# Query rope's weights in the pairs' ring, projections by halves, and the first weights on another queue

## The chip, the cores and the metric

The kernel runs on one core of one Trainium2 chip. The metric is the device time of one execution in microseconds. Five engines run their own instruction streams: TensorE (PE, matmuls; PEld is its weight load), VectorE (DVE), ScalarE (ACT), GpSimd (POOL) and SyncE (SP, which mostly issues DMAs). They meet through semaphores. Matmuls read from SBUF and write to PSUM banks, and a bank can be written again only when its last reader is done.

## The reference

Input x is 1024 tokens by 1024 features. Layer 1 is a gated linear recurrence, layer 2 is attention whose keys and values come from one shared low-rank projection. All in float32. In outline:

```python
# layer 1
u = rms_norm(x) @ w_in;  xb, gate = split(u)            # 1280 + 1280
xb = causal_conv(xb);    r, i = sigmoid gates per block of 128
h = associative_scan(exp(-8 r softplus(-lam)), ...)
x = x + (h * silu(gate)) @ w_out
# shared keys and values
ckr = rms_norm(x) @ w_dkv;  c_kv = rms_norm(ckr[:256]);  k_rope = rope(ckr[256:])
k_nope, v = c_kv @ w_uk, c_kv @ w_uv                    # 8 heads of 128
# layer 2
u = rms_norm(x) @ w_in;  c_q = rms_norm(u[:384]);  gate = u[384:]
q = c_q @ w_uq;  q_nope, q_rope = q[:128], rope(q[128:])  # per head
o = causal softmax(scale * (q_nope k_nope + q_rope k_rope)) @ v
x = x + (o * silu(gate)) @ w_out;  out = rms_norm(x, final_norm)
```

## The kernel before, in words

**Three matmuls for one product.** Every float32 operand is split into a high part (rounded for the fast matmul format) and a low part: the helper `hl` (lines 81 to 83) rounds on ACT (L82) and subtracts on DVE (L83). A product is the sum of three matmuls, high by high, high by low, low by high (`mm3`, L114 to L116). Tiles `wh`, `wl` are the parts of a weight, `pg` is a page of 128 by 1024 (one of 36), `wr` the raw weight, `ps` and `pm` PSUM banks, `s` the scores' banks, `pt` the transposed probabilities.

**The start.** Eighteen small matmuls on ones (L285) keep PE running until data are there. SP, ACT and DVE follow a hand-written order here (`manual_schedule`): SP issues the halves of x's first pages (`xload`, L245) and the first weights (`Weights.load`, L267) in turn; ACT loads its function table (L288), then scales and splits each piece of x (L252, DVE's half is L253) and adds up the squares (L275, L277, DVE L149); the sum reaches PE as the matmul of L359.

**The pairs.** From about 365 to 525 us, the projections into keys, queries and gates run as products of two row blocks at a time in Strassen's manner: `pair` makes seven products (`fmul`) of 12 matmuls into four banks a, b, c, d, where copies of banks (`copy`, ACT L634) start other banks: b starts from a's content, cc keeps c, d starts from b, v2 keeps b. Differences go through DVE (L654). Each pair's weights come from four loads of winc (L526) into the ring `wa` of 7 buffers; ACT scales each by four small instructions (L530), DVE adds them to each other (L542), and `hl` splits them into rings `wh` and `wl` of 4. The instructions of a pair's weights and its copies carry a priority (WPRI or WPC, 100 and 120) with which the scheduler places them ahead in the engines' queues; the queues themselves run strictly in order. Query rope (`qrope`) needs four weights of its own (wuqr, 192 KB); they use the general ring `wr` of 2 buffers (`wtile`, L91). The gates' pairs 0, 2, 4 and 6 follow each other, query rope stands after gates pair 2.

**The heads.** From about 527 us, eight heads of eight query blocks each: scores (five matmuls for each piece of 512, L890 to L894) into one of two banks `s`; mask and row maximum on DVE (L895, L897), exponential on ACT (L900), normalisation on DVE (L901, L902); transposes on PE (L910) that are split again into `pt`; and for each half of the queries the product with the values (`pv`, L925 to L927), multiplied by the gate on DVE (L929). The next head's projections `kq` are cut into four pieces, q first and second half, then k first and second half, which a table (KQ_AT, by query block) spreads between the blocks as filler. PVD says how many blocks after its half `pv` is placed: 1, but 3 for the second part of head 6. The last projection and the final norm follow from about 785 us.

Of the kernel before, what the change touches and what calls it, by code (L numbers as in the profile page):

```python
# [10 lines left out]
F32R = mybir.dt.float32r  # L11
# [10 lines left out]
NH = 8  # L22
# [11 lines left out]
DEPQ = "gpsimd"  # L34
LOOK = 2
KQ_AT = (1, 0, 1, 0, 2, 0, 0, 0)
V0_AT = (1, 1, 2, 0)
V_AT = (0, 0, 0, 0, 0, 0, 1, 1)
D_AT = (0, 4, 1, 1, 1, 0, 3, 2)
# [10 lines left out]
GADD = ()  # L50
NWA = 7
WPC = 120


NA, CW, CB, BR, BI, LAM, NKV, KVN, NB, QN, FN, NVEC = 0, 8, 48, 58, 68, 78, 88, 96, 98, 106, 109, 117
# [2 lines left out]
def trunk(tc, xT, wina, vecs, wgate, wouta, winc, wuk, wuv, wuq, wuqr, woutb, rope, outT):  # L58
# [196 lines left out]
    class Weights:  # L255
# [6 lines left out]
            self.lo = wp.tile([P, 4 * P], F32R, tag="wl", bufs=4, name=nm("wl"))  # L262
            ks += [(self.hi[:, k * P:(k + 1) * P], self.lo[:, k * P:(k + 1) * P]) for k in range(4)]

        def load(self, k0=0, k1=4):
            c = slice(k0 * P, k1 * P)
            nc.sync.dma_start(out=self.raw[:, c], in_=self.src[:, c])  # L267

        def split(self, k0=0, k1=4):
            c = slice(k0 * P, k1 * P)  # L270
# [14 lines left out]
        T.matmul(out=warm[:, 0:P], lhsT=onesd, rhs=onesd, start=True, stop=True)  # L285
    rb = accp
    with tc.manual_schedule(engines={_E.SP, _E.Activation, _E.DVE}):
        A.activation(out=atab, in_=onesd[:, 0:1], func=AF.Abs_reciprocal_sqrt)  # L288
        sp = softplus()

        def step(n):
            for _ in range(n):
                next(sp, None)

        w0 = [Weights(wina[j][:, 0:4 * P], w) for j, w in ((0, wx), (NCT, wg))]
        xload(0, hs(0))
        w0[0].load(0, 1)
        w0[1].load(0, 1)
        xload(0, hs(1))
        w0[0].load(1, 4)  # L300
        xload(1, hs(0))
        w0[1].load(1, 4)
        xload(1, hs(1))
        xload(2)
        xload(3)
        step(SPN[0])
        xsplit(0, hs(0))
        w0[0].split(0, 1)
        w0[1].split(0, 1)
        xsplit(0, hs(1))  # L310
        ps0 = [pst() for _ in range(4)]

        def products(k):
            for i in range(4):
                mm3(ps0[i], (wx, wg)[i // 2][k], (xs[k][0][:, hs(i % 2)], xs[k][1][:, hs(i % 2)]), k == 0, k == NKT - 1)

        def first(k):

            for h in range(2):
                for wp_, xp in ((0, 0), (0, 1), (1, 0)) if (k, h) == (0, 0) else ((0, 0), (1, 0), (0, 1)):  # L320
                    for i in range(2):
                        T.matmul(out=ps0[2 * i + h], lhsT=(wx, wg)[i][k][wp_], rhs=xs[k][xp][:, hs(h)],
                                 start=k + wp_ + xp == 0, stop=False)

        first(0)
        w0[0].split(1, 4)
        xsplit(1, hs(0))
        w0[1].split(1, 4)
        xsplit(1, hs(1))
        w4 = [Weights(wina[j][:, 4 * P:], w) for j, w in ((0, wx), (NCT, wg))]  # L330
        for w in w4:
            w.load()
        for k in range(4, NKT):
            xload(k)
        first(1)
        done = 0
        for k in range(2, NKT):
            xsplit(k)
            step(SPN[1])
            if k == 3:  # L340
                for w in w4:
                    w.split()
            products(k)
            while done <= k - SQL:
                squares(done)
                step(SPN[1])
                done += 1
        for k in range(done, NKT):
            squares(k)
        ws = wload(wgate[0], 2 * P, tag="s", pool=ta, rb=1, hb=1)  # L350
        wx = wtile(wina[1], NKT, cast=True)
        ap = [(tt(F32R), tt(F32R)) for _ in range(2)]
        for h in range(2):
            hl(accp[:, hs(h)], *ap[h])
        for h in range(2):
            t1, t2 = tt(), tt()
            ps = pst()
            for i in range(2):
                T.matmul(out=ps, lhsT=onesr, rhs=ap[h][i], start=i == 0, stop=i == 1)  # L359
            newton(rb[:, hs(h)], ps, 1.0 / D, t1, t2)  # L360
        step(99)
# [264 lines left out]
    def pair(m, dst, w, banks, raw=(False, False), mid=None):  # L626

        a, c, b, d = banks
        cc = tcp.tile([P, HW], F32, tag="cc", bufs=2, name=nm("cc"))
        v2 = tcp.tile([P, HW], F32, tag="v2", name=nm("v2"))  # L630

        def copy(dst_, src, scale=1.0):
            with tc.high_priority(offset=WPC):
                A.activation(out=dst_, in_=src, func=AF.Copy, scale=scale)  # L634

        fmul(a, w[0], 0, True)
        copy(b, a, -1.0)
        fmul(c, w[1], 1, True)
        copy(cc, c)
        fmul(b, w[2], 2, False)  # L640
        fmul(a, w[3], 4, False)
        copy(d, b)
        copy(v2, b)
        fmul(d, w[4], 3, False)
        rest = mid() if mid else None

        def put(i, h, src):
            if raw[i]:
                A.activation(out=dst[i][h], in_=src, func=AF.Copy)
            else:  # L650
                byr(dst[i][h], src, r1[:, hs(h)])

        def put2(i, h, x, y):
            V.tensor_tensor(out=dst[i][h], in0=x, in1=y, op=ALU.subtract)  # L654
            if not raw[i]:
                byr(dst[i][h], dst[i][h], r1[:, hs(h)])

        put2(1, 1, d, cc)
        put(0, 0, a)
        fmul(c, w[5], 6, False)  # L660
        put2(0, 1, c, v2)
        fmul(d, w[6], 5, False)
        put(1, 0, d)
        if rest:
            rest()

    def wa():
        return tcp.tile([P, HW], F32, tag="wa", bufs=NWA, name=nm("wa"))
# [108 lines left out]
    qsd = dp.tile([4, 2 * P, S], F32, name="qsd")  # L777

    def qrope(g):
        wab = [wtile(wuqr[2 * g + i], 3) for i in range(2)]  # L780
        for h in range(2):
            pA, pB = pst(), pst()
            mmt(pA, wab[0], cq, hs(h))
            mmt(pB, wab[1], cq, hs(h))
            for c, (o1, o2, op) in enumerate(((cs, sn, ALU.subtract), (sn, cs, ALU.add))):
                t1, t2 = tk(), tk()
                V.tensor_tensor(out=t1, in0=pA, in1=o1[:, hs(h)], op=ALU.mult)
                V.tensor_tensor(out=t2, in0=pB, in1=o2[:, hs(h)], op=ALU.mult)
                V.tensor_tensor(out=t1, in0=t1, in1=t2, op=op)
                th, tl = parts(t1, t2.bitcast(F32R))  # L790
                DQ.dma_start(out=qsd[c, g * P:(g + 1) * P, hs(h)], in_=f(th))
                DQ.dma_start(out=qsd[2 + c, g * P:(g + 1) * P, hs(h)], in_=f(tl))
# [47 lines left out]
    def kq(hd):  # L840

        wk, wq = wtile(wuk[hd], 2), wtile(wuq[hd], 3)
        k, q = (page(), page()), (page(), page())
        qs = tp.tile([P, S], F32R, tag="qs", name=nm("qs")) if hd else page()
        for c in range(4):
            nc.sync.dma_start(out=f(qs[32 * c:32 * c + 32, :]), in_=qsd[c, 32 * hd:32 * hd + 32, :])

        def proj(w, src, dst, h):
            ps = pm()
            mmt(ps, w, src, hs(h))  # L850
            hl(ps, dst[0][:, hs(h)], dst[1][:, hs(h)])

        work = [lambda a=a, h=h: proj(*a, h) for a in ((wq, cq, q), (wk, ckv, k)) for h in range(2)]
        return (k, q, qs), work

    def vals(pair, half):
# [124 lines left out]
    for i, (hd, qb) in enumerate(items):  # L981
        if qb == 0:
            gt = page(F32)
            nc.sync.dma_start(out=gt, in_=gd[hd])
            gates.append(gt)
            if hd + 1 < NH:
                heads[hd + 1], kqwork = kq(hd + 1)
        if qb == VQB and hd // 2 + 1 < NH // 2:
            vwork += vals(hd // 2 + 1, hd % 2)
        if i + LOOK < len(items):  # L990
            nh = items[i + LOOK]
            if nh[1] == 0 and nh[0]:
                while kqwork:
                    kqwork.pop(0)()
            pend[nh] = scores(*nh, *heads[nh[0]])
        if i == 8 * (NH - 1) + DSTART:
            dwork = [lambda a=a: dpart(*a) for a in DPART]
        for wl, n in ((kqwork, KQ_AT[qb]), (vwork, V0_AT[qb] if hd == 0 and qb < 4 else V_AT[qb]), (dwork, D_AT[qb - DSTART] if i >= 8 * (NH - 1) + DSTART else 0)):
            for _ in range(min(n, len(wl))):
                wl.pop(0)()  # L1000
        g = qb // 4
        if qb % 4 == 0:
            pts[hd, g] = [tuple(tp.tile([P, 4, HW], F32R, tag=f"pt{i}", name=nm("pt")) for i in range(2)) for _ in range(g + 1)]

        if late and i - late[0][0] >= (PVD if (hd, qb) < (NH - 2, 4) or hd == NH - 1 else 3):
            pv(*late.pop(0)[1:])
        transposes(qb, pend.pop((hd, qb)), pts[hd, g])
        if qb % 4 == 3:
            late.append((i, hd, g, pts.pop((hd, g))))
        j = i - 8 * (NH - 1)  # L1010
        for _ in range(YL_AT.count(j)):
            yload(ny)
            ny += 1
        for _ in range(WOUT_AT.count(j)):
            wout(len(wob))
# [131 lines left out]
```

## Time and profile before

| | |
|---|---|
| median of 3 runs | 873.49 us (873.47 to 873.86) |
| the profiled execution's own time | 873.94 us |
| its span, first to last instruction | 872.2 us |
| PE busy | 856.4 us, 4326 matmuls |
| DVE busy | 660.7 us |
| ACT busy | 519.1 us |
| granted clock of TensorE | 0.996 |

The span is 1.74 us shorter than the execution's own time; what lies around it is outside the profile. Rows of a timeline read: start, length, engine, line, operation, output and inputs, shape, and in brackets how long the engine had been idle and what released it. PE's rows show modelled ends: a matmul of 512 columns is shown with 0.39 us though the next starts 0.23 us after it.

### The profile page before, as it was taken

What the parts mean: (1) busy time and instruction counts of PE and PEld (TensorE: products, weight loads), DVE (VectorE), ACT (ScalarE), POOL (GpSimd) and SP (SyncE); (2) the same over time, 40 slices, a digit from 0 to 9 for tenths busy, and PEclk for the clock granted to TensorE, in tenths of its full rate; (3) what the DMA queues carried; (4) which work ended last, traced back from release to release, by engine and by line L of the source; (5) the groups of instructions that cost most, each with busy time, mean ns of one, the idle gap of its engine ahead of it and who ended that gap; (6) DMA issues with size and microseconds to landing.
All of it is one profiled execution on the core that took longest, in us unless ns stands there. A gap on an engine that the chain in (4) does not pass through costs nothing.

```text
span 872.2 us, 12195 instructions
## 1 busy us (share of the span) xinstructions
PE 856.4 (98%) x4326; PEld 728.3 (84%) x4326; DVE 660.7 (76%) x1227; ACT 519.1 (60%) x961; POOL 73.3 (8%) x143
## 2 busy tenths in 40 slices
PE   9999999999999999999999999999999999999995
PEld 6788888888888888888778889988998998888995
DVE  6988788777877774779878957887797887875353
ACT  7567787776787543699875545555565554431222
POOL 1001110011000100001211320000000000010000
PEclk9999999999999999999999999999999999999998
DMA  8333333333212544133544674122231326666032
GB/s 294 94 97 97 97 96 98 107 100 95 79 37 91 169 151 158 49 109 122 182 138 170 204 257 133 52 83 96 70 112 67 105 74 249 217 211 216 14 130 75
DMA packets 52222, 109.00 MB, mean 125 GB/s; under 512 B 6593, under 2 KB 17217, under 8 KB 52161
## 3 DMA queue, kind: packets, MB, share of 16 engines
q1 hardware_dynamic: 36400, 67.19, 23.7%
q0 software_dynamic: 15216, 40.51, 13.9%
q8 instruction: 34, 0.56, 0.3%
q10 hardware_dynamic: 544, 0.52, 0.2%
q14 instruction: 28, 0.22, 0.1%
HBM read 81.46 MB, written 26.21 MB: 123 GB/s over the span
## 4 chain that ended last, share of the span: by engine, by line
PE 88%; DVE 4%; ACT 3%; DMA 2%; issue 2%; SPq 0%; POOL 0%; DVEq 0%; ACTq 0%; POOLq 0%
PE ps L114 16%; PE ps L116 16%; PE ps L115 16%; PE pm L116 6%; PE pm L115 6%; PE pm L114 6%; PE pm L910 3%; PE pm L926 2%; PE pm L927 2%; PE s L891 2%; PE pm L925 2%; PE s L893 2%; PE s L894 2%; PE s L892 2%; PE s L890 2%
## 5 line engine op out<-in xcount | busy, mean ns | idle before, releaser
L114 PE MATMUL ps<-pg,wh 128*128 128x512 f32 x664 | 257.1, 390 | 3.3 <-ACT ps L634 2.4
L115 PE MATMUL ps<-pg,wh 128*128 128x512 f32 x664 | 258.7, 390 | 0.6 <-DVE pg L253 0.5
L116 PE MATMUL ps<-pg,wl 128*128 128x512 f32 x664 | 258.4, 389 | 0.0
L114 PEld LDWEIGHTS ps<-pg,wh 128*128 128x128 f32 x664 | 124.6, 188 | 31.0 <-ACT ps L634 3.6
L115 PEld LDWEIGHTS ps<-pg,wh 128*128 128x128 f32 x664 | 124.6, 188 | 27.7 <-DVE pg L253 1.9
L116 PEld LDWEIGHTS ps<-pg,wl 128*128 128x128 f32 x664 | 124.6, 188 | 25.9
L82 ACT ACTIVATE pt<-pm 128x512 fp32r<-128x512 f32 (+2 forms) x96 | 44.3, 490 | 59.4 <-PE pm L910 54.5
L900 ACT ACTIVATE pg<-s,m 128x128 f32<-128x128 f32 (+3 forms) x64 | 47.4, 742 | 45.1 <-DVE m L897 40.4
L114 PE MATMUL pm<-pg,pg 128*128 128x256 f32 (+1 forms) x192 | 61.9, 322 | 0.0
L115 PE MATMUL pm<-pg,pg 128*128 128x256 f32 (+1 forms) x192 | 61.6, 321 | 0.0
L116 PE MATMUL pm<-pg,pg 128*128 128x256 f32 (+1 forms) x192 | 61.4, 320 | 0.0
L83 DVE TENSOR_TENSOR pt<-pm,pt 128x512 fp32r<-128x512 f32 (+2 forms) x96 | 50.5, 548 | 2.3 <-ACT pt L82 2.2
L897 DVE TENSOR_REDUCE m<-s 128x1 f32<-128x128 f32 (+3 forms) x64 | 48.2, 754 | 1.1
L82 ACT ACTIVATE wh<-wr 128x512 fp32r<-128x512 f32 (+3 forms) x59 | 31.2, 531 | 26.0 <-PE ps L115 15.2
L83 DVE TENSOR_TENSOR wl<-wr,wh 128x512 fp32r<-128x512 f32 (+3 forms) x59 | 33.1, 564 | 16.1 <-ACT wh L82 15.9
L381 DVE SCALAR_TENSOR_TENSOR t<-xb,vec,t 128x512 f32<-128x512 f32 x60 | 44.8, 747 | 0.4
L82 ACT ACTIVATE pg<-pg 128x512 fp32r<-128x512 f32 x42 | 26.1, 630 | 30.0 <-DVE pg L435 18.3
L910 PE MATMUL pm<-ident,pg 128*128 128x128 f32 x288 | 42.3, 274 | 0.7 <-DVE pg L929 0.7
L116 PE MATMUL pm<-pg,wl 128*128 128x512 f32 x108 | 42.3, 392 | 0.0
L115 PE MATMUL pm<-pg,wh 128*128 128x512 f32 x108 | 42.3, 392 | 0.0
L114 PE MATMUL pm<-pg,wh 128*128 128x512 f32 x108 | 42.1, 390 | 0.0
L114 PEld LDWEIGHTS pm<-pg,pg 128*128 128x128 f32 x192 | 36.6, 191 | 2.6 <-issue 0.2
(232 smaller groups left out, 1803.4 us busy)
## 6 DMA issues: line engine op xcount, KB each, us to landing
wr<-wina SPq DMA_DIRECT2D x38, 256.0 KB, 2.9
wh<-wina POOLq DMA_DIRECT2D x36, 256.0 KB, 2.9
wa<-winc SPq DMA_DIRECT2D x24, 256.0 KB, 3.1
ysd<-pg POOLq DMA_DIRECT2D x12, 512.0 KB, 3.2
pg<-ysd SPq DMA_DIRECT2D x12, 512.0 KB, 8.9
wr<-wouta SPq DMA_DIRECT2D x16, 256.0 KB, 2.7
t<-xT SPq DMA_DIRECT2D x16, 256.0 KB, 3.4
x1d<-t POOLq DMA_DIRECT2D x16, 256.0 KB, 2.5
```

The source lines that it names most:

```text
L82: A.activation(out=hi, in_=src, func=AF.Copy)
L83: V.tensor_tensor(out=lo, in0=src, in1=f(hi), op=ALU.subtract)
L114: T.matmul(out=ps, lhsT=w[0], rhs=r[0], start=first, stop=False, skip_group_check=more)
L115: T.matmul(out=ps, lhsT=w[0], rhs=r[1], start=False, stop=False, skip_group_check=more)
L116: T.matmul(out=ps, lhsT=w[1], rhs=r[0], start=False, stop=last, skip_group_check=more)
L381: V.scalar_tensor_tensor(out=xc, in0=xb[:, j:j + HW], scalar=cwv[j], in1=xc, op0=ALU.mult, op1=ALU.add)
L890: T.matmul(out=sc[:, c], lhsT=q[0][:, ql], rhs=k[0][:, c], start=True, stop=False)
L891: T.matmul(out=sc[:, c], lhsT=q[0][:, ql], rhs=k[1][:, c], start=False, stop=False)
L892: T.matmul(out=sc[:, c], lhsT=q[1][:, ql], rhs=k[0][:, c], start=False, stop=False)
L897: V.tensor_reduce(out=m, in_=sc, axis=AX.X, op=ALU.max, negate=True)
L900: A.activation(out=p_[:, 0:nk], in_=sc, func=AF.Exp, bias=m, accum_out=l)
L910: T.transpose(out=ps[:, (b - b0) * P:(b - b0 + 1) * P], in_=p_[:, b * P:(b + 1) * P], identity=ident)
```

## The change

Four edits, all of order and placement; the matmuls are the same.

1. The first two weight loads (64 KB each) are issued by ACT, ahead of its table load, and no longer by SP between the pieces of x.
2. The copies of banks in `pair` get priority 600 in place of 120.
3. Query rope's weights are taken from the pairs' ring `wa`, by code that repeats `wtile`'s split.
4. A head's projections come as q, k of the first half, then q, k of the second. For the last head, the second halves are left until after its first scores (table KQ_LAST), and `pv` stands one block after its half everywhere.

```diff
+KQ_LAST = (1, 0, 0, 0, 1, 0, 1, 1)
+WPB = 600
...
-        def load(self, k0=0, k1=4):
+        def load(self, k0=0, k1=4, q=nc.sync):
             c = slice(k0 * P, k1 * P)
-            nc.sync.dma_start(out=self.raw[:, c], in_=self.src[:, c])
+            q.dma_start(out=self.raw[:, c], in_=self.src[:, c])
...
+        w0 = [Weights(wina[j][:, 0:4 * P], w) for j, w in ((0, wx), (NCT, wg))]
+        for w in w0:
+            w.load(0, 1, nc.scalar)
         A.activation(out=atab, in_=onesd[:, 0:1], func=AF.Abs_reciprocal_sqrt)
...
-        w0 = [Weights(wina[j][:, 0:4 * P], w) for j, w in ((0, wx), (NCT, wg))]
         xload(0, hs(0))
-        w0[0].load(0, 1)
-        w0[1].load(0, 1)
         xload(0, hs(1))
...
-            with tc.high_priority(offset=WPC):
+            with tc.high_priority(offset=WPB):
                 A.activation(out=dst_, in_=src, func=AF.Copy, scale=scale)
...
     def qrope(g):
-        wab = [wtile(wuqr[2 * g + i], 3) for i in range(2)]
+
+        wab = []
+        for i in range(2):
+            with tc.high_priority(offset=WPRI):
+                raw = wa()[:, 0:3 * P]
+                hi = wp.tile([P, 3 * P], F32R, tag="wh", bufs=4, name=nm("wh"))
+                lo = wp.tile([P, 3 * P], F32R, tag="wl", bufs=4, name=nm("wl"))
+                nc.sync.dma_start(out=raw, in_=wuqr[2 * g + i])
+                hl(raw, hi, lo)
+            wab.append([(hi[:, k * P:(k + 1) * P], lo[:, k * P:(k + 1) * P]) for k in range(3)])
...
-        work = [lambda a=a, h=h: proj(*a, h) for a in ((wq, cq, q), (wk, ckv, k)) for h in range(2)]
+        work = [lambda a=a, h=h: proj(*a, h) for h in range(2) for a in ((wq, cq, q), (wk, ckv, k))]
...
-                while kqwork:
+
+                while len(kqwork) > (2 if nh[0] == NH - 1 else 0):
                     kqwork.pop(0)()
...
-        for wl, n in ((kqwork, KQ_AT[qb]), (vwork, V0_AT[qb] if hd == 0 and qb < 4 else V_AT[qb]), (dwork, D_AT[qb - DSTART] if i >= 8 * (NH - 1) + DSTART else 0)):
+        for wl, n in ((kqwork, (KQ_LAST if hd == NH - 2 else KQ_AT)[qb]), (vwork, V0_AT[qb] if hd == 0 and qb < 4 else V_AT[qb]), (dwork, D_AT[qb - DSTART] if i >= 8 * (NH - 1) + DSTART else 0)):
...
-        if late and i - late[0][0] >= (PVD if (hd, qb) < (NH - 2, 4) or hd == NH - 1 else 3):
+        if late and i - late[0][0] >= PVD:
             pv(*late.pop(0)[1:])
```

Two lines more stand at the kernel's head, so L634 becomes L636, and from `qrope` on the lines move by 11 (L929 becomes L940).

The order on ACT around copy d of the first gates pair (the bank ps_3931, L634; L530 scales a winc tile, `wh_...<-wa_...` splits one). Before:

```order
L634 ACTIVATE cc_3932<-ps_3929 128x512
L82 ACTIVATE wh_3920<-wa_3904 128x512
L530 ACTIVATE wa_4433<-wa_4433,vec 128x128 x4
L82 ACTIVATE wh_3924<-wa_3883 128x512
L634 ACTIVATE ps_3931<-ps_3930 128x512
```

Now:

```order
L636 ACTIVATE cc_3932<-ps_3929 128x512
L84 ACTIVATE wh_3920<-wa_3904 128x512
L84 ACTIVATE wh_3924<-wa_3883 128x512
L636 ACTIVATE ps_3931<-ps_3930 128x512
L636 ACTIVATE v_775_3933<-ps_3930 128x512
```

The four scalings of wa_4433 have left this place; they now stand before the split of wh_4141 that is followed by copy d of gates pair 2 (ps_4148), where those of wa_4602 stood. On SP, the loads of that stretch before:

```order
L526 DMA wa_4121<-winc 128x512
L91 DMA wr_4253<-wuqr 128x384
L526 DMA wa_4433<-winc 128x512
L526 DMA wa_4439<-winc 128x512
L526 DMA wa_4445<-winc 128x512
L526 DMA wa_4466<-winc 128x512
L91 DMA wr_4259<-wuqr 128x384
L526 DMA wa_4602<-winc 128x512
```

Now:

```order
L528 DMA wa_4121<-winc 128x512
L789 DMA wa_4253<-wuqr 128x384
L789 DMA wa_4259<-wuqr 128x384
L789 DMA wa_4341<-wuqr 128x384
L789 DMA wa_4347<-wuqr 128x384
L528 DMA wa_4433<-winc 128x512
L528 DMA wa_4439<-winc 128x512
L528 DMA wa_4445<-winc 128x512
```

All four wuqr loads now stand ahead of the winc loads of gates pair 4 (wa_4433 and on). On PE in head 6, from the end of block 4's scores (s_7196) to the scores of block 5, before:

```order
L894 MATMUL s_7196<-pg_4776,qs_6749 128x256
L114 MATMUL pm_7215<-pg_4062,wh_7101 128x512
L115 MATMUL pm_7215<-pg_4063,wh_7101 128x512
L116 MATMUL pm_7215<-pg_4062,wl_7102 128x512
L114 MATMUL pm_7215<-pg_4068,wh_7101 128x512
L115 MATMUL pm_7215<-pg_4069,wh_7101 128x512
L116 MATMUL pm_7215<-pg_4068,wl_7102 128x512
L114 MATMUL pm_7215<-pg_4074,wh_7101 128x512
L115 MATMUL pm_7215<-pg_4075,wh_7101 128x512
L116 MATMUL pm_7215<-pg_4074,wl_7102 128x512
L910 MATMUL pm_7227<-ident,pg_7124 128x128 x3
L890 MATMUL s_7233<-pg_6745,pg_6747 128x512
```

Now:

```order
L904 MATMUL s_7196<-pg_4775,qs_6749 128x256
L905 MATMUL s_7196<-pg_4776,qs_6749 128x256
L921 MATMUL pm_7215<-ident,pg_7124 128x128 x3
L901 MATMUL s_7221<-pg_6745,pg_6747 128x512
L902 MATMUL s_7221<-pg_6746,pg_6747 128x512
```

The nine matmuls of the second half of q have left this place; with the six of k's second half they follow the first scores of head 7.

## The prediction

> **What bounds the kernel now.** I read the page first, then busy time by stretch, then TensorE's waits, then the timelines around each wait.
>
> ```profile
> span 872.2 us, 12195 instructions
> PE 856.4 (98%) x4326; PEld 728.3 (84%) x4326; DVE 660.7 (76%) x1227; ACT 519.1 (60%) x961; POOL 73.3 (8%) x143
> ...
> PE 88%; DVE 4%; ACT 3%; DMA 2%; issue 2%; SPq 0%; POOL 0%; DVEq 0%; ACTq 0%; POOLq 0%
> ```
>
> TensorE (PE) is busy 98% of the span and 88% of the chain that ended last is its own work. The change removes no matmul, so all it can win is PE's idle time. Where that lies, by stretch (columns: length, then PE, PEld, DVE, ACT, POOL busy, granted clock, DMA share, GB/s):
>
> ```profile
> 1.70:4.60 2.90, 2.90 (x15) 2.90 (x15) 0.90 (x7) 0.95 (x3) 0.00 (x0) 1.00 0.67 197
> 4.60:14.00 9.40, 8.86 (x34) 5.84 (x33) 5.61 (x9) 6.95 (x12) 0.00 (x0) 1.00 0.98 331
> ...
> 427.00:460.00 33.00, 29.66 (x127) 23.25 (x126) 27.59 (x45) 27.05 (x60) 4.37 (x8) 1.00 0.39 127
> 460.00:742.00 282.00, 282.00 (x1592) 248.32 (x1591) 228.47 (x479) 154.78 (x337) 25.77 (x48) 1.00 0.38 130
> 742.00:748.00 6.00, 4.93 (x34) 4.24 (x34) 5.82 (x15) 4.12 (x12) 0.53 (x1) 1.00 1.04 398
> ```
>
> Between 460 and 742 us, as an example of the rest, PE never idles. Where the change works it idles in three places: the start, 427 to 460 us (3.34 us idle: the pairs of products), and 742 to 748 us (1.07 us: the end of head 6). PE's own waits name the releasers:
>
> ```profile
> PE ps L114 <- ACT ps L634: 2.4, 3, 1.1
> ...
> PE ps L114 <- DVE tk L654: 1.0, 1, 1.0
> PE pm L910 <- DVE pg L929: 0.7, 1, 0.7
> ```
>
> So three waits for ScalarE's bank copies (L634), one for VectorE's difference (L654), one for its product with the gate (L929) at the end of head 6. A shown wait is too short, because matmuls of 512 columns start every 0.23 us while a row shows 0.39; I therefore measure a stall from start to start, less 0.23, plus 0.11 because the first row after a stall lasts 0.50 and not 0.39.
>
> **The pairs' stretch, 427 to 460 us.** Timelines of ACT and of PE (start, length, operation, idle before it and its releaser):
>
> ```profile
> 420.90 0.60 ACT L649 ACTIVATE pg<-ps 128x512 f32<-128x512 f32 x1 [1.79 <-DMA kvd<-pg]
> ```
>
> ```profile
> 428.30 0.39 PE L116 MATMUL ps<-pg,wl 128*128 128x512 f32 x1
> 429.67 0.50 PE L114 MATMUL ps<-pg,wh 128*128 128x512 f32 x1 [0.98 <-ACT ps L634]
> ```
>
> Stall A, 1.37 − 0.23 + 0.11 = 1.25 us, is the first gates pair's copy b. It runs late because ACT was held 1.79 us by a spill to DRAM (kvd). The change moves nothing ahead of that, so I leave A: 0, at best −0.6 if the spill lands early.
>
> ```profile
> 434.16 1.28 ACT L530 ACTIVATE wa<-wa,vec 128x128 f32<-128x128 f32 x4 [0.72 <-DMA wa<-winc]
> ...
> 435.86 0.57 ACT L634 ACTIVATE ps<-ps 128x512 f32<-128x512 f32 x1
> ```
>
> ```profile
> 435.04 0.39 PE L116 MATMUL ps<-pg,wl 128*128 128x512 f32 x1
> ...
> 436.49 0.50 PE L114 MATMUL ps<-pg,wh 128*128 128x512 f32 x1 [1.07 <-ACT ps L634]
> ```
>
> Stall B, 1.45 − 0.23 + 0.11 = 1.33 us, is copy d of the same pair. ACT stood 0.72 us for a weight load and then spent 1.28 us on four scalings of it (wa_4433, weights of a pair 45 us ahead), and copy d was queued behind them. In the new order those four are no longer there: the four wuqr loads now take the ring's places first, so wa_4433's buffer and its scalings come a pair later. Without them ACT reaches copy d, now at 435.86, 0.72 + 1.28 us earlier, at about 433.9, done by 434.5; PE wants it at 435.04 + 0.23 = 435.27. B goes whole: **−1.33**. Copy priorities alone (WPB) would not have done it, since the order shows only two other copies trading places, where PE has no stall.
>
> ```profile
> 441.17 0.69 DVE L83 TENSOR_TENSOR wl<-ws,wh 128x512 fp32r<-128x512 f32 x1 [1.37 <-ACT wh L82]
> ...
> 446.11 0.68 DVE L654 TENSOR_TENSOR tk<-ps,cc 128x512 f32<-128x512 f32 x1
> ```
>
> ```profile
> 445.50 0.39 PE L116 MATMUL ps<-pg,wl 128*128 128x512 f32 x1
> 446.85 0.50 PE L114 MATMUL ps<-pg,wh 128*128 128x512 f32 x1 [0.96 <-DVE tk L654]
> ```
>
> Stall C, 1.35 − 0.23 + 0.11 = 1.23 us, hangs on DVE's L654, which ends at 446.79 after ten operations back to back since 441.17. That first one waited 1.37 us for a split on ACT, again queued behind scalings of winc tiles that the new order takes away. Without them the split waits only for its buffer, which PE frees at the end of the product that stall B delayed, so at about 438.2; DVE starts near 438.9 and L654 ends near 444.5. PE, 1.33 us earlier, arrives at 445.73 − 1.33 = 444.40. That is a tie: I take **−1.1**, between −0.6 (DVE half a microsecond later) and −1.23.
>
> ```profile
> 456.01 1.28 ACT L530 ACTIVATE wa<-wa,vec 128x128 f32<-128x128 f32 x4 [1.70 <-DMA wa<-winc]
> ...
> 457.72 0.58 ACT L634 ACTIVATE ps<-ps 128x512 f32<-128x512 f32 x1
> ```
>
> ```profile
> 457.64 0.39 PE L116 MATMUL ps<-pg,wl 128*128 128x512 f32 x1
> 458.35 0.50 PE L114 MATMUL ps<-pg,wh 128*128 128x512 f32 x1 [0.33 <-ACT ps L634]
> ```
>
> Stall D is copy d of the second gates pair, again behind four scalings, which waited 1.70 us for a load: 0.71 − 0.23 + 0.11 = 0.59 us. The new order still puts four scalings there (now wa_4433's). Their load is released by VectorE's split after a product of PE, so it moves forward with PE and does not fall behind by what B and C give. It also no longer shares the engines with a 192-KB wuqr load issued just ahead. Between nothing and all of it: **−0.45**.
>
> The other qrope costs: the four wuqr loads go out earlier on SP and their tiles sit in the ring until split. PE has no wait from 460 to 742 us, so the cover there is the weights' lead over their products; I add nothing, and the price if it runs out is a rival below.
>
> **The start.** SP's issues of the two first-weight loads and of the next piece of x, then where ACT's and PE's chain begins and ends:
>
> ```profile
> 1.66 0.90 SPq L267 DMA_DIRECT2D wr<-wina  x2
> 2.60 0.43 SPq L245 DMA_DIRECT2D pg<-xT  x1
> ```
>
> ```profile
> 10.97 1.15 ACT L252 ACTIVATE pg<-pg,vec 128x1024 fp32r<-128x1024 f32 x1 [0.53 <-DMA pg<-xT]
> ```
>
> ```profile
> 31.66 0.50 PE L359 MATMUL ps<-t,onesr 128*128 128x512 f32 x1 [0.46 <-DVE t L83]
> ```
>
> PE's stalls up to 31.66 all wait for the splits of x, and these run almost back to back on ACT and DVE from x2's landing (10.97) to the wait at 31.66. Moving the two first-weight DMAs to ACT takes 2.60 − 1.66 = 0.94 us out of SP's queue ahead of everything behind them. The engines stand idle for 0.33 × 2.90 = 0.96 us from 1.70 to 4.60, and are at 0.98 after that, so x2 lands at most about 0.95 us earlier and at least not later than now. I take **−0.75**, nearer the upper end, because the idle share lies exactly where the issues were slow. ACT's table load comes two issues later, which the wait for x0 hides.
>
> A rule speaks against this part: the Trainium skill, "DMA: Bandwidth & Descriptors", section "Issuing engines are not separate DMA queues", says that DMAs of all issuing engines run on the same 16 DMA engines and interleave, so a second queue saves issue time only. By the 0.98 after 4.60 us the trace agrees. If that held already for the first transfers, this term would be 0 and the sum smaller by 0.75, which is the first rival.
>
> **The heads.** The halves' order puts six matmuls (k, first half) instead of nine (q, second half) ahead of the block-5 scores of heads 1 to 6. Those scores wait for a bank that the exponential of block 3 frees:
>
> ```profile
> 571.85 0.69 ACT L900 ACTIVATE pg<-s,m 128x512 f32<-128x512 f32 x1 [0.92 <-DVE m L897]
> ```
>
> ```profile
> 574.12 0.48 PE L890 MATMUL s<-pg,pg 128*128 128x512 f32 x1
> ```
>
> Three matmuls are 0.68 us, and PE had 574.12 − (571.85 + 0.69) = 1.58 us in hand, so 0.90 is left: no cost. In head 6 nothing stands there any more, since its second halves go behind the last head's first scores, and these rows give the price:
>
> ```profile
> 726.82 0.69 ACT L900 ACTIVATE pg<-s,m 128x512 f32<-128x512 f32 x1 [0.92 <-DVE m L897]
> ```
>
> ```profile
> 726.78 0.40 PE L114 MATMUL pm<-pg,wh 128*128 128x512 f32 x1
> ...
> 728.84 0.49 PE L910 MATMUL pm<-ident,pg 128*128 128x128 f32 x3
> 729.09 0.48 PE L890 MATMUL s<-pg,pg 128*128 128x512 f32 x1
> ...
> 743.06 0.28 PE L894 MATMUL s<-pg,qs 128*128 128x256 f32 x1
> 744.08 1.42 PE L910 MATMUL pm<-ident,pg 128*128 128x128 f32 x11 [0.74 <-DVE pg L929]
> ...
> 746.46 0.27 PE L910 MATMUL pm<-ident,pg 128*128 128x128 f32 x1
> 747.07 0.50 PE L926 MATMUL pm<-pt,pg 128*128 128x512 f32 x1 [0.33 <-DVE pt L83]
> ```
>
> PE reached that point at 726.78 and did products for 2.06 us; now the three transposes (729.09 − 728.84 = 0.25) follow at once and then the scores, at 727.03, whose bank is free at 726.82 + 0.69 = 727.51: a new stall of 0.48 + 0.11 = 0.59 us. Against it stands stall E: 1.02 − 0.12 = 0.90 us at 743.06, where a transpose needs the bank that the value product (pv) of head 6 held until L929, and 0.61 − 0.11 + 0.11 = 0.61 at 746.46. With pv earlier and the moved products ahead as filler, both go: −1.51 + 0.59 = **−0.9**, from −0.4 (half of E stays) to −1.5 (no new stall).
>
> Sum: −0.75 − 1.33 − 1.1 − 0.45 − 0.9 = −4.5 us, from the profiled 873.94 to 869.4. That run lies 0.45 above the median of 873.49, so the median comes to **869.0**; my own range about it is 868.2 to 869.9. A difference under 0.2%, 1.75 us here, cannot be told from none.
>
> **The rivals.**
> 1. The start is bound by bytes and D stays: −4.5 + 0.75 + 0.45 = −3.3, so 870.2. For it: the share of 0.98. Against: 0.96 us of idle before it.
> 2. C stays a wait (its buffer is freed by PE, its ten operations keep their length) and half a microsecond of E as well: 1.1 + 0.5 back, −2.9, so 870.6. For it: the tie at 444.4. Against: the ten operations have no idle among them that could grow.
> 3. More than I count: A shrinks with the earlier start, all bounds at their good ends: −0.95 − 1.33 − 1.23 − 0.59 − 1.5 − 0.6 = −6.2, so 867.3. Against: nothing of A's cause is moved.
> 4. The change does not do what it says: what B and C give back is waited for at D, because the load there is bound by its own length and not by PE. Then only the start and E count, −1.65: 871.8, which is no difference. Against: the split that releases the load follows PE's product.
> 5. Slower: the halves' order costs a stall in each of heads 1 to 6. If the moved splits stand ahead of the block-3 exponential by three VectorE operations of 0.68, it ends 2.04 later; less the 0.90 in hand, plus 0.11, that is 1.25 a head and 7.5 in all: −4.5 + 7.5 = +3.0, so 876.5. It decides from 0.90 us of lateness on, and outweighs the rest from 1.6. Against: in the order the same splits stand at that place as before.
>
> **Chances.** Forecast 55%; rivals 1 to 5: 15%, 12%, 10%, 5%, 3%. The range reaches to rival 3 and to rival 2 with some rest: 867.3 to 871.0. Faster by over 0.2% (below 871.74) hold the forecast and rivals 1 to 3: 92%; the same 5%; slower 3%.
>
> **What would show it.** In the profile after: PE's waits for ACT's L636 down from three to one or two, the one at A left with about 1 us; none for DVE's L656 over 0.3; no wait for L940 in head 6, but one of about half a microsecond on the scores after block 4; the wait of L361's matmul 0.7 to 0.9 us earlier in time; the scalings of wa_4433 directly ahead of the second pair's copy d. It is wrong if the stretch of the pairs still shows over 2 us idle, or if any wait appears between 460 and 740 us other than that in head 6.

## The result and the profile after

The changed kernel takes 867.73 us (median of 5 runs, 867.47 to 868.37); the kernel before took 873.55 in the same comparison (5 runs, 873.47 to 873.94). The ratio is 0.9934, with a 95% interval of 0.9919 to 0.9948: 5.8 us less. Forecast were 869.0, in a range of 867.3 to 871.0. The profiled execution is one at the fast end, 867.47 us with a span of 865.7.

TensorE's waits in the profile after, all that the list shows:

```profile
PE ps L287 <- DVE onesd L135: 1.1, 1, 1.1
PE pm L1090 <- ACT sq L1086: 0.5, 1, 0.5
PE ps L324 <- ACT wh L84: 0.5, 1, 0.5
PE ps L361 <- DVE t L85: 0.5, 1, 0.5
PE ps L117 <- DVE pg L255: 0.4, 1, 0.4
PE s L901 <- ACT pg L911: 0.4, 1, 0.4
```

The three waits for the bank copies (before L634, now L636) are gone, all three, and so are those for L656 and L940. The last row is new: the block-5 scores of head 6. Busy time in the same stretches as in the prediction:

```profile
1.70:4.60 2.90, 2.90 (x15) 2.90 (x15) 0.90 (x7) 1.51 (x3) 0.00 (x0) 1.00 0.95 256
4.60:14.00 9.40, 8.89 (x39) 6.77 (x38) 6.82 (x11) 8.47 (x13) 0.00 (x0) 1.00 1.01 355
...
427.00:460.00 33.00, 33.00 (x146) 27.07 (x145) 31.61 (x52) 26.35 (x54) 5.21 (x10) 1.00 0.47 147
460.00:742.00 282.00, 281.62 (x1600) 248.19 (x1599) 229.11 (x485) 156.49 (x347) 25.58 (x48) 1.00 0.38 127
742.00:748.00 6.00, 6.00 (x35) 5.36 (x35) 4.23 (x11) 1.58 (x4) 0.00 (x0) 1.00 1.06 408
```

The pairs' stretch is full (33.00 of 33.00 us busy, where 29.66 were), and so is the end of head 6. In the start the DMA engines are busy from 1.70 us on, at 0.95 where it was 0.67. Its issues, x2's first scaling and the end of the wait that closes the start, from the timelines of ACT, SP and PE:

```profile
0.74 0.91 ACTq L269 DMA_DIRECT2D wr<-wina  x2
...
9.59 1.15 ACT L254 ACTIVATE pg<-pg,vec 128x1024 fp32r<-128x1024 f32 x1 [0.74 <-DMA pg<-xT]
```

```profile
1.19 0.91 SPq L247 DMA_DIRECT2D pg<-xT  x2
```

```profile
30.30 0.50 PE L361 MATMUL ps<-t,onesr 128*128 128x512 f32 x1 [0.46 <-DVE t L85]
```

And the new stall in head 6, PE:

```profile
721.00 0.49 PE L921 MATMUL pm<-ident,pg 128*128 128x128 f32 x3
721.86 0.50 PE L901 MATMUL s<-pg,pg 128*128 128x512 f32 x1 [0.38 <-ACT pg L911]
```

Both halves of x's first page now go out at once, while ACT issues the weights; x2 is scaled 1.38 us earlier. The scores of block 5 stand behind three transposes and wait. Measured as in the prediction, start to start, the two profiles differ by this:

| place | before, us | after, us | difference | forecast |
|---|---|---|---|---|
| start: the wait of L359, now L361, ends at | 31.66 | 30.30 | −1.36 | −0.75 |
| stall A (copy b) | 1.25 | 0 | −1.25 | 0 |
| stall B (copy d) | 1.33 | 0 | −1.33 | −1.33 |
| stall C (difference) | 1.23 | 0.11 | −1.12 | −1.1 |
| stall D (copy d of the next pair) | 0.59 | 0 | −0.59 | −0.45 |
| stall E and the new one (head 6) | 1.51 | 0.65 | −0.86 | −0.9 |
| sum | | | −6.5 | −4.5 |

The spans differ by 872.2 − 865.7 = 6.5 us, so nothing is left over. These two executions differ by more than the medians do (6.5 against 5.8).

### The profile page after: what moved, and what is told of

Same layout as the page of the kernel before. It is cut to its first block, busy times and chain, and to the rows that moved or that the text cites. A ratio compares the mean times of both kernels' runs of the same rounds, so it can differ in the third digit from the quotient of the medians.

```text
span 865.7 us, 12199 instructions
## 1 busy us (share of the span) xinstructions
PE 854.0 (99%) x4326; PEld 728.3 (84%) x4326; DVE 660.9 (76%) x1227; ACT 518.3 (60%) x961; POOL 73.6 (9%) x143
## 4 chain that ended last, share of the span: by engine, by line
PE 95%; DVE 2%; issue 1%; DMA 1%; ACT 1%; SPq 0%; DVEq 0%
PE ps L117 18%; PE ps L116 18%; PE ps L118 18%; PE pm L118 6%; PE pm L116 6%; PE pm L117 6%; PE pm L921 4%; PE pm L937 2%; PE pm L938 2%; PE s L904 2%; PE s L905 2%; PE s L903 2%; PE s L902 2%; PE s L901 2%; PE pm L936 2%
## 5 line engine op out<-in xcount | busy, mean ns | idle before, releaser
L84 ACT ACTIVATE wh<-wr 128x512 fp32r<-128x512 f32 (+3 forms) x55 | 29.0, 531 | 24.5 <-PE ps L117 11.9
L85 DVE TENSOR_TENSOR wl<-wr,wh 128x512 fp32r<-128x512 f32 (+3 forms) x55 | 30.5, 566 | 14.3 <-ACT wh L84 14.1
```

What stands on the lines that cost most here:

```text
L84: A.activation(out=hi, in_=src, func=AF.Copy)
L85: V.tensor_tensor(out=lo, in0=src, in1=f(hi), op=ALU.subtract)
```

## The experiments

**The four edits apart.** The kernel before with one edit each. First the start:

```diff
+        w0 = [Weights(wina[j][:, 0:4 * P], w) for j, w in ((0, wx), (NCT, wg))]
+        for w in w0:
+            w.load(0, 1, nc.scalar)
         A.activation(out=atab, in_=onesd[:, 0:1], func=AF.Abs_reciprocal_sqrt)
...
-        w0[0].load(0, 1)
-        w0[1].load(0, 1)
```

> The kernel before with the first-weight edit alone. Theory (issue time plus better use of the engines before 4.6 us): the wait of L361's matmul moves from 31.66 to about 30.3 us, x2's first scaling from 10.97 to about 9.6 us, stalls A to E stay as they were (A 1.25, B 1.33, C 1.23, D 0.59 us), time -1.4 us against the kernel before. Rival (the issue slots alone, 0.94 us): x2's scaling at about 10.0, time -0.9 or less. Rival on A (it went because everything starts earlier): A is under 0.3 us here, time -2.6.

Measured: 872.49 us against 873.66, ratio 0.999 (0.9981 to 0.9999): −1.2 us. In its profile L359's wait ends at 30.79 (0.9 earlier) and x2's first scaling starts here:

```profile
10.08 1.15 ACT L252 ACTIVATE pg<-pg,vec 128x1024 fp32r<-128x1024 f32 x1 [0.55 <-DMA pg<-xT]
```

That is 0.89 us earlier than before, nearer the rival's figure (the issue slots, 0.94) than the theory's. Stall A is 0.84 us here and C 1.65: the earlier start alone does not end A. As with the copies and the heads below, the gain is under 0.2% and the interval only just excludes none; what each edit does is read from its profile.

Second, the copies' priority:

```diff
-            with tc.high_priority(offset=WPC):
+            with tc.high_priority(offset=WPB):
                 A.activation(out=dst_, in_=src, func=AF.Copy, scale=scale)
```

> The kernel before with the copies' priority 600 alone. Theory (the two copies of the pair at 414 us now precede a weight split on ACT, so VectorE makes the low parts of two spilled key pages before its share of that split, and the spill that held ACT lands earlier): the wait on the spill falls from 1.79 us to about 0.75, stall A from 1.25 us to under 0.2, B to E stay or take up part of it, time -1.2 us at most. Rival (priority costs and gives nothing, as I predicted): A stays 1.25 us, time within 0.2 us of before.

Measured: 872.37 us, ratio 0.9983 (0.9974 to 0.9992): −1.3 us. Stall A is gone, B 0.90 and C 1.25 stay, D is not there. How it works is to be seen on VectorE. In the kernel before (timeline from 413 us):

```profile
413.94 0.69 DVE L83 TENSOR_TENSOR pg<-pg,tk 128x512 fp32r<-128x512 f32 x1
414.54 0.69 DVE L83 TENSOR_TENSOR wl<-wa,wh 128x512 fp32r<-128x512 f32 x1
415.14 1.89 DVE L83 TENSOR_TENSOR pg<-pg,tk 128x512 fp32r<-128x512 f32 x3
```

With the copies' priority:

```profile
413.79 1.89 DVE L84 TENSOR_TENSOR pg<-pg,tk 128x512 fp32r<-128x512 f32 x3
415.60 0.68 DVE L84 TENSOR_TENSOR wl<-wa,wh 128x512 fp32r<-128x512 f32 x1
416.20 0.68 DVE L84 TENSOR_TENSOR pg<-pg,tk 128x512 fp32r<-128x512 f32 x1
```

`pg<-pg,tk` are the low parts of four half pages (the two pages of c_kv), each of which is then spilled to DRAM (kvd); `wl<-wa,wh` is the low part of a weight. On ACT two copies now precede that weight's split, so on DVE its low part comes two places later, and the low parts of the second and third half page come 0.6 us earlier in their row. GpSimd issues the spills. Before:

```profile
414.92 0.54 POOL L744 DMA_DIRECT2D kvd<-pg  x1 [0.38 <-DVE pg L83]
416.13 1.75 POOL L744 DMA_DIRECT2D kvd<-pg  x3 [0.66 <-DVE pg L83]
```

With the copies' priority:

```profile
414.77 1.75 POOL L745 DMA_DIRECT2D kvd<-pg  x3 [0.38 <-DVE pg L84]
417.18 0.54 POOL L745 DMA_DIRECT2D kvd<-pg  x1 [0.66 <-DVE pg L84]
```

ACT's L649 (L650 in this experiment, L651 in the changed kernel) waits for the second of these spills. In the trace of the kernel before it is issued at 416.13 us and lands at 420.81; here it is issued at 415.37 and lands at 419.79. Of the shorter wait the place in the row accounts for 0.6 us; the rest is a landing after 4.4 us where it was 4.7. ACT's row in this experiment:

```profile
419.87 0.60 ACT L650 ACTIVATE pg<-ps 128x512 f32<-128x512 f32 x1 [0.91 <-DMA kvd<-pg]
```

0.91 us of waiting, where it was 1.79, and TensorE has no stall at copy b.

Third, the ring:

```diff
-        wab = [wtile(wuqr[2 * g + i], 3) for i in range(2)]
+        wab = []
+        for i in range(2):
+            with tc.high_priority(offset=WPRI):
+                raw = wa()[:, 0:3 * P]
...
```

> The kernel before with query rope's weights in the pairs' ring alone. Theory: stall B (1.33 us) gone, C (1.23) down to about 0.1, D (0.59) gone, A stays 1.25; time -3.0 us. Rival (D takes up what B and C give): D over 1.5 us, time -1 us or less.

Measured: 871.39 us, ratio 0.9973 (0.9964 to 0.9983): −2.3 us. Of the pairs' stretch only A is left, with 1.27 us:

```profile
428.72 0.39 PE L116 MATMUL ps<-pg,wl 128*128 128x512 f32 x1
430.11 0.50 PE L114 MATMUL ps<-pg,wh 128*128 128x512 f32 x1 [1.00 <-ACT ps L634]
```

B, C and D are gone, so nothing that B and C gave was taken up at D. The time fell by less than the 3.0 expected, most of all because D, 0.59 of it, is not in the other profiles with the old ring (see below).

Fourth, the heads (halves' order, KQ_LAST, and the value product one block after its half):

```diff
+KQ_LAST = (1, 0, 0, 0, 1, 0, 1, 1)
...
-for a in ((wq, cq, q), (wk, ckv, k)) for h in range(2)]
+for h in range(2) for a in ((wq, cq, q), (wk, ckv, k))]
...
-                while kqwork:
+                while len(kqwork) > (2 if nh[0] == NH - 1 else 0):
...
-        if late and i - late[0][0] >= (PVD if (hd, qb) < (NH - 2, 4) or hd == NH - 1 else 3):
+        if late and i - late[0][0] >= PVD:
```

> The kernel before with the halves' order, the last head's late halves and the value product one block after its half. Theory: E's two stalls (1.51 us) gone, one new stall of about 0.6 us at the block-5 scores of head 6, time -0.8 us; heads 1 to 5 without any stall. Rival (the halves' order costs in each head): stalls at the block-5 scores of heads 1 to 5 of 0.2 us or more each.

Measured: 872.87 us, ratio 0.999 (0.998 to 0.9999): −0.8 us. E is gone, and one new stall of 0.65 us stands at the block-5 scores of head 6; heads 1 to 5 have none. The four add up to −1.17 − 1.29 − 2.27 − 0.79 = −5.5, against −5.8 together. With intervals of about 0.8 us to either side for each, no interaction between them is to be seen.

**The changed kernel once more, and without the copies' priority.** The second has one edit:

```diff
-WPB = 600
+WPB = 120
```

> The changed kernel once more, for a second profile and as the base of the three others: time -5.8 us against the kernel before, x2's first scaling between 9.6 and 10.1 us, stall A under 0.7 us, B and D none, C under 0.3, one stall of about 0.6 at the block-5 scores of head 6.

> The changed kernel with the copies' priority back at 120. Theory (A's end comes from the copies' order): the wait on the spill is back at 1.4 us or more, stall A at 0.7 us or more, time +0.7 to +1.3 us against the changed kernel. Rival (A's end comes from the earlier start or from the ring): A under 0.3, time as the changed kernel.

Measured: 868.07 us (867.84 to 868.19, 4 runs) and 869.45 (868.58 to 870.6). Stall A is back, at TensorE and at its cause on ACT:

```profile
426.97 0.39 PE L118 MATMUL ps<-pg,wl 128*128 128x512 f32 x1
428.24 0.50 PE L116 MATMUL ps<-pg,wh 128*128 128x512 f32 x1 [0.89 <-ACT ps L636]
```

```profile
419.46 0.60 ACT L651 ACTIVATE pg<-ps 128x512 f32<-128x512 f32 x1 [1.62 <-DMA kvd<-pg]
```

1.27 − 0.23 + 0.11 = 1.15 us of stall, 1.62 of waiting, and 1.4 us of time. So A's end is due to the copies' order, with and without the other edits. The repeated profile of the changed kernel has no stall in the pairs' stretch (33.00 of 33.00 busy), and L361's wait ends at 30.86: the start gave 0.80 us there, 1.36 in the first.

**Is it the order of x and the weights, or the second queue?** All on SP, x's first page ahead of the first weights:

```diff
         xload(0, hs(0))
+        xload(0, hs(1))
         w0[0].load(0, 1)
         w0[1].load(0, 1)
-        xload(0, hs(1))
```

> The kernel before with both halves of x's first page issued ahead of the two first-weight loads, all on SP: the same order of transfers on SP as in the change up to there, but no second queue and no issue slot saved. If the second queue matters (slots, and fuller engines): x2's first scaling at about 11.0 us and 310 to 330 GB/s from 4.6 to 9.6 us as before, time within 0.3 us of before or later, since the first product waits for its weights. If the order of x and weights matters: x2 at 10.1 or earlier, over 350 GB/s, time -0.9 us.

Measured: 873.86 us, ratio 1.0002 (0.9992 to 1.0011): nothing. x2's first scaling is at 11.30 us and the engines move 283 GB/s from 4.6 to 9.6 us. The engines' share from 1.70 to 4.60 us rose to 0.81 (0.67 before), but x2's load is issued where it was, at 4.98 us. So neither the order of x and the weights nor fuller engines at the start gives the gain; moving the issues off SP does. Then two more loads (192 KB each) to ACT's queue, on top of the kernel of the next paragraph, which is its base:

```diff
             w.load(0, 1, nc.scalar)
+        for w in w0:
+            w.load(1, 4, nc.scalar)
...
-        w0[0].load(1, 4)
...
-        w0[1].load(1, 4)
```

> The same with the next two weight loads (192 KB each) on ACT's queue too. If SP's issue slots set x2's landing: another 0.94 us, x2 at about 9.1 us, time -0.9 us more. If bytes set it from here on (the engines are at 0.92 to 0.97 from 1.7 us on): x2 no earlier than 9.6, and x0 may land later because the weights of the second queue come between; time within 0.3 us of the base, or later by up to 0.5.

Measured: 867.59 us (866.97 to 868.11) against its base's 867.09 (866.82 to 867.92): no gain, x2's first scaling at 9.95 us, DMA share 0.92 from 1.70 to 4.60. The same loads stand ahead of x2 as in the base. By the traces x2 is issued at 3.40 us where the base has 4.04, and lands at 9.92 where the base has 9.46: here the further issue slots on SP are worth nothing.

**The new stall.** The changed kernel with k's first half of the last head two blocks earlier:

```diff
-KQ_LAST = (1, 0, 0, 0, 1, 0, 1, 1)
+KQ_LAST = (1, 0, 1, 0, 0, 0, 1, 1)
```

> The changed kernel with the last head's first half of k placed two blocks earlier (ahead of the block-5 scores of head 6). Theory (the new stall is lack of filler): the 0.65 us at those scores go, time -0.6 us against the changed kernel if nothing lacks the six matmuls where they were taken away. Rival (the lack moves along): a stall of 0.4 us or more at the transposes or scores of blocks 4 to 7, time as the changed kernel.

> The changed kernel with the first half of k two blocks earlier, again, as the base of the next kernel and with more rounds: time -6.3 us against the kernel before, x2's first scaling between 9.6 and 10.3 us, no stall from 32 to 800 us over 0.2.

Measured: 867.26 us (867.07 to 867.55), beside 868.07 (867.84 to 868.19) of the changed kernel on the same chip: 0.8 us less, and the two sets of runs do not overlap. A second comparison gave 867.09 (ratio to the kernel before 0.9928, 0.9916 to 0.994). Its busy time from 32 to 800 us:

```profile
32.00:800.00 768.00, 768.00 (x3778) 651.52 (x3777) 607.66 (x1125) 479.60 (x899) 70.22 (x131) 1.00 0.38 126
```

TensorE is never idle there: the stall is gone and has not moved. This is the fastest kernel of the study.

**The two halves of the heads' edit apart.** The value product alone:

```diff
-        if late and i - late[0][0] >= (PVD if (hd, qb) < (NH - 2, 4) or hd == NH - 1 else 3):
+        if late and i - late[0][0] >= PVD:
```

> The kernel before with the value product of head 6 one block after its half, as elsewhere, and nothing else. Theory (both of E's waits come from the bank and the transposed block that the late value product holds): both go, no stall at the block-5 scores since the nine matmuls still stand there, time -1.5 us. Rival (the late halves are needed as filler): one of E's stalls stays or a new one of 0.5 us or more comes before 750 us, time -0.8 or less.

Measured: 873.65 us, ratio 1.0002 (0.9992 to 1.0011): no gain. E's two waits are gone, but two others stand at the same place:

```profile
743.70 0.39 PE L890 MATMUL s<-pg,pg 128*128 128x256 f32 x1 [0.94 <-ACT pg L900]
...
744.84 0.41 PE L910 MATMUL pm<-ident,pg 128*128 128x128 f32 x2 [0.28 <-DVE pg L902]
```

Now the scores of the next head wait for a bank that the exponential holds. The halves without the value product, KQ_LAST and the order of the pieces:

```diff
+KQ_LAST = (1, 0, 0, 0, 1, 0, 1, 1)
...
-for a in ((wq, cq, q), (wk, ckv, k)) for h in range(2)]
+for h in range(2) for a in ((wq, cq, q), (wk, ckv, k))]
...
-                while kqwork:
+                while len(kqwork) > (2 if nh[0] == NH - 1 else 0):
```

> The kernel before with the halves' order and the last head's late halves, the value product left where it was. Theory: the new stall of 0.65 us at head 6's block-5 scores comes, E's stalls shift but stay for the most part (over 0.7 us in all), time 0 to -0.5 us. Rival (the filler in head 7 is what ends E): E's 1.51 us gone, time -0.8.

Measured: 873.29 us, ratio 0.9998 (0.9989 to 1.0007): no gain either. The new stall of 0.65 us comes, and E leaves two short waits, one of them this:

```profile
746.45 0.50 PE L891 MATMUL s<-pg,pg 128*128 128x512 f32 x1 [0.25 <-ACT pg L901]
```

Neither part shows a gain alone; together they give 0.8 us. The intervals of these two times reach 0.7 to 0.9 us below no gain, so it is the waits in the profiles that carry this, more than the times: about as much stall as E's 1.51 us stands in each. The value product frees the bank, and the moved halves put work where TensorE would wait for the next one.

## Why the prediction was right, and where it was not

The time of 867.73 us lies inside the range given (867.3 to 871.0), but below the narrower one about the forecast (868.2 to 869.9). The range had been drawn down to rival 3, which gave stall A 0.6 us for another cause than the one found, so that A's gain still falls inside it is partly luck. Without A the forecast fits: the changed kernel without the copies' priority took 869.45 us, 869.0 were forecast, with a start sized too low and a D sized too high making up for each other.

**What bounds it** was right: all of the gain is TensorE's idle time in the three stretches named, and the table's sum equals the difference of the spans.

**B** was right in size and cause (1.33 of 1.33): the ring alone removes it, and copy d then runs without a wait.

**C** was the tie that the prediction called: what is left of it is the 0.11 us of a restart. VectorE's difference in the profile after:

```profile
441.03 0.69 DVE L656 TENSOR_TENSOR tk<-ps,cc 128x512 f32<-128x512 f32 x1
```

It ended at 441.72, and TensorE's product started at 441.77. The prediction had 444.5 and 444.4; both are earlier by what the start and A gave (1.36 + 1.25).

**A** was wrong. The step that failed is "The change moves nothing ahead of that". The sentence that the copies' priority "would not have done it, since the order shows only two other copies trading places, where PE has no stall" was written of B, and of B it is right (0.90 us with that edit alone); but the same reading, that such a trade is without effect because PE has no stall there, seems to stand behind leaving A at 0. The two copies moved ahead of a weight's split on ACT, so that split's second half moved back on DVE; in front of it came the low parts that are spilled, and behind the spill stood the ACT instruction that made copy b late. The stall lies 14 us after the trade, on another engine's queue. The edit was worth −1.3 us by itself and its removal +1.4. Rival 3 gave A 0.6 us for another cause, the earlier start. That does not end A: with the early start and without the priority A is 0.84 and 1.15 us. These are the two smallest of the eight profiles without the priority (the other six have 1.25 to 1.67), so that it shrinks A a little is neither shown nor excluded.

**The start** had the right cause and was sized too low. The gain was set at 0.75 and capped at 0.95, the issue time saved. x2's first scaling came at 10.97, 11.03, 11.38, 11.04, 11.41 and 10.91 us in the six profiles with the old start (the order experiment apart) and at 9.59, 10.08, 10.16, 9.63, 10.26 and 9.48 in six with the new (the one with two more loads apart): 11.12 and 9.87 on average, 1.26 us. SP's issues of three loads of x, of which x2 is the second, before and after:

```profile
4.50 1.38 SPq L245 DMA_DIRECT2D pg<-xT  x3
```

```profile
3.57 1.45 SPq L247 DMA_DIRECT2D pg<-xT  x3
```

By the traces x2's load is issued at 4.98 us in the six and at 4.02 to 4.04 in the other six, so the saved issue time counts in full, 0.95 us. The other 0.3 us is the time from issue to landing, 6.1 us before and 5.8 after on average (5.91 to 6.40 and 5.42 to 6.21 in single profiles); what shortens it, the second queue or something else, was not separated. Rival 1, that bytes bind already and the start gives nothing, did not happen; what it describes fits the run in which two more loads are moved. The Trainium skill's rule ("DMA: Bandwidth & Descriptors", "Issuing engines are not separate DMA queues") agrees with that last run and with the 0.95 us: a second queue saves issue time, and beyond that the 867.59 us against 867.09 show nothing. The 0.3 us goes beyond the rule. Since it is issue time that was saved, the rule did not speak against this term, as the prediction had it.

**D** had its cause right, but should have been near 0 on average. It stands only in the first profile of the kernel before, where ACT waited 1.70 us for that load; it waited 0.32 to 1.09 us in the six later profiles with the old ring (the start, copies, heads, order, value-product and halves experiments), and none of them shows the stall. One execution's stall was priced at 0.45 of its 0.59 us, as if most executions had it. The same spread shows in A, between 0.84 and 1.67 us in profiles that have it, and in B, between 0.78 and 1.45, with C mostly larger where B is smaller.

**E** came out as worked (−0.86 for −0.9), the new stall with 0.65 for 0.59. The slack in heads 1 to 6 was read rightly: no stall in heads 1 to 5 in any of the runs with the halves' order. Rival 5 did not occur, nor did rival 4, as the ring alone shows.

So the sum was short by A (1.25) and by 0.4 to 0.6 us of the start, and long by D in most profiles; the total, −4.5 against −5.8, has the right parts but for A.

## What to carry to other kernels

When an order changes on one engine, follow each moved instruction to the other engines and through their DMAs, and not only to the place where it stands: a trade of two places was worth 1.3 us 14 us later. A small wait on a shared resource that depends on how a DMA landed should be looked for in more than one execution before it is priced. And where a wait names a bank, ask what the engine would wait for next: moving the value product alone, or the filler alone, left about as much stall as before, both together did not.

## What the runs showed of the hardware that was not expected

At nearly the same busy share of the DMA engines the rate differed by a sixth: 0.96 with 318 GB/s from 4.6 to 9.6 us before, 1.01 with 372 after. More than half of that is the place of the window: the loads from x2 on are issued about 0.95 us earlier after the change, and the kernel before, looked at 0.95 us later, shows 356 GB/s, again at 0.96.

```profile
4.60:9.60 5.00, 4.58 (x19) 3.09 (x17) 3.33 (x7) 3.19 (x7) 0.00 (x0) 1.00 0.96 318
```

```profile
5.55:10.55 5.00, 4.58 (x18) 2.95 (x18) 3.03 (x8) 3.12 (x6) 0.00 (x0) 1.00 0.96 356
```

```profile
4.60:9.60 5.00, 4.49 (x21) 3.49 (x20) 4.17 (x8) 4.07 (x9) 0.00 (x0) 1.00 1.01 372
```

The first two rows are the kernel before, the third the changed one. Over the six profiles with the old start and the six with the new, the averages in the order of these rows are 308, 340 and 366 GB/s. Between 4.6 and 9.6 us the first trace has 129 packets of 4 KB, the changed kernel's 235, and in both a packet of 4 KB took 159 ns (median), one of 2 KB 84, one of 512 bytes 27: the larger ones move more in the same time, so a share near 1 does not fix the rate.

The wait for a spill of 256 KB to DRAM was 1.36 to 2.21 us in the eight profiles without the copies' priority, all with the same order around it, and 0.75 to 0.93 in the six with it.
